# Two heads' small products alternate between the halves of TensorE's array, and a low part is laid out on all rows

## The chip, the cores and the metric

The kernel runs on one core of one Trainium2 chip. The metric is device time in microseconds of one launch, weights read from HBM included. Everything is float32 at the interface. TensorE's array has 128 rows (the contraction) and 128 columns (the outputs' partitions); an instruction whose operands need only 64 rows or 64 columns is placed on one half of the array. A stationary operand is loaded by a weight load (PEld in the profile), and a matmul then streams the moving operand past it.

## The reference

Three transformer blocks for 512 tokens of width 1024. The first two mix three branches, and the third has attention, a delta rule and an expert layer:

```python
def first_block(x, p, ...):
    for i in range(2):
        h = rms_norm(x, norm_g[i]); z = h @ w_in[i]
        y_a = rwkv7_branch(z_a, ...)      # 6 heads of 64
        y_b = dsa_branch(z_b, ...)        # 4 heads, top 128 keys by an index score
        y_c = dilated_branch(z_c, ...)    # 3 groups of 2 heads, banded windows
        x = x + concat(y_a, y_b, y_c) @ w_out[i]
        x = x + sigmoid(rms_norm(x, ple_norm_g[i]) @ ple_w_gate[i]) * (p[i] @ ple_w_proj[i])
    return rms_norm(x, final_norm_g)

def second_block(x, c, ...):
    h = rmsnorm(x, n1) * (1 + sc1) + sh1
    # block_attention: softmax(q k^T / 8) v, 8 query heads on 2 key heads of 64
    # gated_delta_chunked: 8 heads of 64, forward and backward; per chunk (k b)(k^T) and q k^T
    x = x + gt1 * ((gate_a * (attn @ w_attn_up) + gate_d * (dn @ w_dn_up)) @ w_o)
    return x + gt2 * expert_choice_ffn(...)   # 16 experts, 64 tokens each
```

Every head has 64 features, so a score product contracts over 64 rows, and P V makes 64 output rows.

## The kernel before

Two heads share one tile of 128 partitions: head e = 0 lies on partitions 0 to 63 and head e = 1 on 64 to 127. Scores of a head therefore use 64 rows of the array (the half that belongs to the head), and P V, which contracts over 128 keys, writes 64 partitions and uses 64 columns (again the head's half).

The places that the change touches:

- `emit_rwkv` (L493), first branch, six times (two layers, three head pairs): Gram products of keys, 64 rows, 256 moving columns, four matmuls for each of two sources and two chunk pairs.
- `emit_dil` (L655, L656), three groups, four blocks, two heads: scores, then a mask added through an identity in bfloat16. `dil_out` (L706) makes the P V of the same.
- `emit_dsa` (L622, L623, L630): the same with 128 to 512 keys.
- `emit_delta` (L1075): Gram products of the delta rule, four times (p = 0 to 3, a pair of heads each).
- `emit_gqa` (L1208, L1209, L1216): grouped attention, one chunk of two query heads for each p; for each of four blocks of 128 tokens and each head, the scores in two passes (the keys' high part on all rows against the query's high and low part, then the keys' low part on the head's own 64 rows), softmax, four transposes (`attend`, L607) and four P V products.

A float32 matmul is two passes in the trace, each with a weight load of its own; a float32r one (scores of the grouped attention, `K.mm` at L199) is one, and so is a transpose. The order of instructions on each engine is made by a scheduler from the order of the code, the dependencies and the pools' buffers: `emit_delta` calls `between(p)` after the solver's code, and the scheduler merges the grouped attention and the gates' projections (L199) with the solver (`K.solve`, L323, L362), whose float16 products come four at a time, and with the delta rule's state chain behind it (L1109 to L1149). Score tiles `bs`, outputs `bo`, Gram tiles `bg` and transposes `bt` have two PSUM buffers each.

The expert weights' loads wait for marks that stand behind the attention and the delta rule:

```python
d = self.nc.sync.dma_start(t, src)
if first:
    self.after(d, self.mark if self.wmn < NE + NW + NM1 else self.mark2)
```

Of the kernel before, what the change touches and what calls it, by code (L numbers as in the profile page):

```python
# [8 lines left out]
F32 = mybir.dt.float32  # L9
F32R = mybir.dt.float32r  # L10
BF16 = mybir.dt.bfloat16
# [3 lines left out]
ALU = mybir.AluOpType  # L15
# [20 lines left out]
# first-block feature-major chunk order  # L36
C_IQ, C_IK, C_WD, C_RK, C_DQ, C_DG, C_DIL = 0, 2, 3, 4, 16, 18, 20
# column offsets in the constants
# [12 lines left out]
# per-partition vectors of a layer  # L51
# [15 lines left out]
class Block:  # L67
# [33 lines left out]
    def small(self, tag, n, bufs=1):  # L101
        """a [128, n] piece of one tile that holds the short vectors, round robin per tag"""
# [8 lines left out]
    def load_x(self, src, mark=None):  # L111
        """the residual stream, token-major: from DRAM"""
# [12 lines left out]
    def load_c(self, g, t):  # L125
        """constants of one phase; the other phase's take the same place"""
        self.cst[g] = t[:, 0:_CSTS[g]]
        self.nc.scalar.dma_start(self.cst[g], self.a[g])
# [4 lines left out]
    def dense(self, lhs, src, out, bytok=False):  # L133
        """token-major products of a feature-major lhs [k][128, 512] with src [1024, 1024], by halves of its columns;
        out(t, hf, psum); the second half, and with bytok the first, goes token tile by token tile"""
# [31 lines left out]
    # ---- weights: one ring of [128, 1024] tiles  # L167
# [10 lines left out]
    def w(self, src, k=1, name="w", bufs=NS, mark=None):  # L178
        """a [128, 1024] tile of weights (seen as k blocks of columns) in two parts"""
# [4 lines left out]
    def split(self, pool, t, name, shape=(128, 512), eng=None, bufs=None, mark=None):  # L184
        """t = hi + lo exactly, both of the tensor engine's single-pass float32 width"""
# [10 lines left out]
    def mm(self, out, a, b, start, stop):  # L196
        """out += a^T b for operands in two parts"""
# [3 lines left out]
    def wm(self, src, pool):  # L201
        """expert weights: the ring and what the earlier phases have left"""
# [20 lines left out]
    def sumsq(self, sp, t, hf):  # L223
        """sum of squares of half a row tile of the residual stream"""
# [8 lines left out]
    def rstd(self, t):  # L233
        """1 / sqrt(mean of squares + 1e-6) of the rows of tile t"""
# [7 lines left out]
    def row(self, lp, src, name, mark=None):  # L242
        """a row of 1024 on all partitions"""
# [6 lines left out]
    def norm_T(self, sp, hp, scale, bias=None, rs=None):  # L250
        """the rows x * rstd * scale + bias transposed, in two parts: [k][128, 512]"""
# [16 lines left out]
    def tpose(self, src):  # L268
        """four [128, 128] blocks transposed"""
# [5 lines left out]
    def fm(self, hT, wt, pool=None):  # L275
        """a feature-major chunk of a projection: [128 features, 512 tokens] in PSUM"""
# [5 lines left out]
    def rope_fm(self, sp, b, cos, sin, mask, out, perm=None, half=None, scale=1.0):  # L282
        """out = (b * cos + shuffled(b) * sin) * scale; half: one half of b's rows for both halves of out"""
# [16 lines left out]
    def rsqrt(self, out, src, scale, bias):  # L300
        """1 / sqrt(src * scale + bias)"""
# [3 lines left out]
    def silu2(self, out, src, sp, tag, n=512):  # L305
        """out = 2 * silu(src)"""
# [4 lines left out]
    # ---- (I + A)^-1 R for strictly triangular A, four units at a time  # L311
# [1316 lines left out]
```

## Time and profile before

| | |
|---|---|
| runs | median 2271.3 us of 3 (2269.49 to 2281.24) |
| profiled execution, span | 2273.9 us |
| TensorE busy | 2128.9 us, 94% of the span |
| VectorE, ScalarE, GpSimd busy | 1258.6, 980.0, 429.6 us |
| granted TensorE clock, mean | 0.973 of full speed |

The profiled execution is known by its span alone, and that lies 2.6 us above the median of the runs and inside their range. Busy shares are of the whole span; the stages differ, so a change is weighed with the rows of the stage in which it lies. A matmul's duration in the trace includes the time in which its results drain, so the cost of one in a stream is the distance from its start to the next one's start. Where several of one kind follow each other, the timeline gives one row for them, with the first start and the number.

### The profile page before, as it was taken

How to read it: one execution, taken by the hardware profiler on the slowest of the kernel's cores; microseconds unless marked ns; L12 is line 12 of the kernel's file. 1: busy time of each engine (PE TensorE's matmuls, PEld its weight loads, DVE VectorE, ACT ScalarE, POOL GpSimd, SP SyncE). 2: the span in 40 equal slices, each digit the busy share in tenths (PEclk: the TensorE clock that was granted, in tenths of full speed). 3: DMA queues.
4: the chain of work that ended last, by engine and by line, in shares of the span. 5: the costliest groups of instructions: out<-in, count | busy, mean ns of one | idle time of the engine just before them, and what ended most of it. 6: DMA issues, size and time to landing. Idle time of an engine off the chain costs nothing. (4 is left out here: it accounts for less than half of the span.)

```text
span 2273.9 us, 31807 instructions
## 1 busy us (share of the span) xinstructions
PE 2128.9 (94%) x12273; PEld 1439.3 (63%) x12273; DVE 1258.6 (55%) x2406; ACT 980.0 (43%) x1849; POOL 429.6 (19%) x344
## 2 busy tenths in 40 slices
PE   6998999999999899999899999999999799999999
PEld 6754667668886676668767777676677444444443
DVE  5688855655569877645867474757464322222221
ACT  4454545444544464444577584857532011101110
POOL 2132233112222323202141140323110000000000
PEclk9999999899999999999999999999999799999999
DMA  6254251043321111034210202011146699999996
GB/s 203 84 171 146 77 168 57 18 158 107 94 87 38 38 38 47 22 124 153 73 51 31 73 20 75 24 61 43 52 157 257 263 401 409 409 409 409 409 409 267
DMA packets 114335, 348.48 MB, mean 153 GB/s; under 512 B 19820, under 2 KB 20604, under 8 KB 114184
## 3 DMA queue, kind: packets, MB, share of 16 engines
q1 hardware_dynamic: 110152, 340.51, 40.7%
q10 hardware_dynamic: 4032, 5.95, 0.8%
q8 instruction: 97, 1.59, 0.3%
q14 instruction: 54, 0.44, 0.1%
HBM read 332.70 MB, written 10.56 MB: 151 GB/s over the span
## 5 line engine op out<-in xcount | busy, mean ns | idle before, releaser
L193 POOL TENSOR_TENSOR wL<-wring,wH 128x1024 fp32r<-128x1024 f32 x68 | 167.2, 2459 | 702.0 <-ACT wH L190 498.8
L190 ACT ACTIVATE wH<-wring 128x1024 fp32r<-128x1024 f32 x137 | 144.1, 1059 | 133.5 <-PE bm L199 96.5
L1387 PE MATMUL bm<-wm,xe 128*64 128x512 f32 x848 | 185.4, 593 | 0.0
L199 PE MATMUL bm<-hT0H,wH 128*128 128x512 f32 x380 | 158.7, 418 | 2.9 <-ACT wH L190 2.9
L199 PE MATMUL bm<-hT1L,wH 128*128 128x512 f32 x380 | 159.8, 421 | 0.0
L199 PE MATMUL bm<-hT0L,wH 128*128 128x512 f32 x380 | 159.6, 420 | 0.0
L199 PE MATMUL bm<-hT0H,wL 128*128 128x512 f32 x380 | 158.6, 417 | 0.0
L199 PE MATMUL bm<-hT1H,wL 128*128 128x512 f32 x380 | 156.5, 412 | 0.0
L199 PE MATMUL bm<-hT1H,wH 128*128 128x512 f32 x380 | 156.0, 411 | 0.0
L1387 PEld LDWEIGHTS bm<-wm,xe 128*64 128x64 f32 x848 | 75.2, 136 | 106.4 <-issue 99.6
L193 DVE TENSOR_TENSOR wL<-wring,wH 128x1024 fp32r<-128x1024 f32 x69 | 92.2, 1337 | 74.4 <-ACT wH L190 66.4
L344 DVE TENSOR_TENSOR Z<-bz,perm 128x512 f16<-128x512 f32 x168 | 108.6, 684 | 36.7 <-PE bz L323 35.6
L1364 DVE TENSOR_SCALAR OH<-phA,perm 128x64 f32<-128x64 f32 x128 | 30.2, 309 | 136.4 <-PE bz L1375 105.7
L1387 PE MATMUL bm<-wm,aT 128*64 128x512 f32 x432 | 102.3, 602 | 0.7
L354 ACT ACTIVATE XX<-bz 128x512 f16<-128x512 f32 x168 | 101.3, 610 | 3.6 <-PE bz L323 3.6
L323 PEld LDWEIGHTS <-XX 128*128 128x128 f16 x1008 | 63.6, 99 | 59.5 <-issue 27.9
L351 ACT ACTIVATE XX<-bz 128x512 f16<-128x512 f32 x140 | 85.2, 608 | 16.7 <-PE bz L323 14.9
L199 PEld LDWEIGHTS bm<-hT0H,wH 128*128 128x128 f32 x380 | 72.8, 192 | 19.4 <-issue 4.2
L199 PEld LDWEIGHTS bm<-hT0L,wH 128*128 128x128 f32 x380 | 72.6, 191 | 17.5 <-issue 5.7
L199 PEld LDWEIGHTS bm<-hT1L,wH 128*128 128x128 f32 x380 | 71.9, 189 | 18.2 <-issue 5.9
L199 PEld LDWEIGHTS bm<-hT1H,wL 128*128 128x128 f32 x380 | 71.9, 189 | 18.1 <-issue 5.3
L199 PEld LDWEIGHTS bm<-hT0H,wL 128*128 128x128 f32 x380 | 72.6, 191 | 15.5 <-issue 3.3
(815 smaller groups left out, 4922.6 us busy)
## 6 DMA issues: line engine op xcount, KB each, us to landing
wm<-in_w_up SPq DMA_DIRECT2D x112, 512.0 KB
wm<-in_w_down SPq DMA_DIRECT2D x108, 512.0 KB
wm<-in_w_gate SPq DMA_DIRECT2D x100, 512.0 KB
wring<-in_win SPq DMA_DIRECT2D x95, 512.0 KB
wring<-in_w_ada SPq DMA_DIRECT2D x48, 512.0 KB
wring<-in_w_gate SPq DMA_DIRECT2D x20, 512.0 KB
wring<-in_w_down SPq DMA_DIRECT2D x20, 512.0 KB
wring<-in_w_out SPq DMA_DIRECT2D x16, 512.0 KB
```

The costliest lines, as they stand in the source:

```text
L190: d = self.A.activation(out=hi, in_=t, func=AF.Copy)
L193: (eng or self.V).tensor_tensor(out=lo, in0=t, in1=hi.bitcast(F32), op=ALU.subtract)
L199: self.T.matmul(out, a[i], b[j], start=(start and n == 0), stop=(stop and n == 2))
L323: T.matmul(b[:, u], lhs[:, u], rhs if len(rhs.shape) == 2 else rhs[:, u], start=True, stop=True)
L344: V.tensor_tensor(out=z, in0=mm(HL[j][0], X[j]), in1=lv(systems[j], l, 0), op=ALU.mult)
L351: A.activation(out=X[j], in_=mm(XT[j], Z[j]), func=AF.Copy)
L354: A.activation(out=XT[j], in_=b, func=AF.Copy)
L1364: V.tensor_scalar(out=y[:, t, 64 * e:64 * e + 64], in0=K.c("iota")[:, 1:65], scalar1=slot[:, t, x:x + 1], scalar2=scale(t, x), op0=ALU.is_ ...
L1387: T.matmul(bb[hf][s], lhs[:, k, s], w[:, hf * 512:(hf + 1) * 512], start=(k == 0), stop=(k == 7))
```

## The change

In all six places the products of the two heads are written alternately (head 0, head 1, head 0, head 1), each on its half of the array; where a score tile was taken for one head at a time, two are taken at once, and P V of both heads stands behind both heads' transposes. In the grouped attention the keys' low part is copied to all 128 rows, one tile per head, and the second pass multiplies it with the query's high and low part on 128 rows, where it used the head's own 64. Comments and doc strings are gone as well, which shifts line numbers.

```diff
@@ emit_rwkv
-                for h in range(2):
-                    b = K.pg.tile([128, 2, 256], F32, name="bg", bufs=2)
-                    for j in range(2):
-                        T.matmul(b[:, j], src[64 * h:64 * h + 64, c0 + j], AR[64 * h:64 * h + 64, c0 + j], start=True, stop=True)
+                bb = [K.pg.tile([128, 2, 256], F32, name="bg", bufs=2) for h in range(2)]
+                for j in range(2):
+                    for b, s in zip(bb, HS):
+                        T.matmul(b[:, j], src[s, c0 + j], AR[s, c0 + j], start=True, stop=True)
+                for h, b in enumerate(bb):
...
+HS = [slice(64 * e, 64 * e + 64) for e in range(2)]
...
@@ emit_dsa
+            ps = [K.ps.tile([128, 512], F32, name="bs", bufs=2)[:, :w] for e in range(2)]
+            for e, s in enumerate(HS):
+                T.matmul(ps[e], q[hp][s, b * 128:(b + 1) * 128], k[s, 0:w], start=True, stop=False)
+            for e in range(2):
+                T.matmul(ps[e], K.identb, am[b][:, :w] if b else K.msk["caus"], start=False, stop=True)
+            PT = []
             for e in range(2):
-                s = slice(64 * e, 64 * e + 64)
-                p = K.ps.tile([128, 512], F32, name="bs", bufs=2)
-                T.matmul(p[:, :w], q[hp][s, b * 128:(b + 1) * 128], k[s, 0:w], start=True, stop=False)
-                T.matmul(p[:, :w], K.identb, am[b][:, :w] if b else K.msk["caus"], start=False, stop=True)
...
-                softmax_parts(K, sp, p[:, :w], w, P, l)
+                softmax_parts(K, sp, ps[e], w, P, l)
...
-                PT = attend(K, sp, P, w, l)
-                for j in range(b + 1):
-                    T.matmul(o[s, b], v[:, j, 0:64], PT[:, j], start=(j == 0), stop=(j == b), skip_group_check=True)
+                PT.append(attend(K, sp, P, w, l))
+            for j in range(b + 1):
+                for e, s in enumerate(HS):
+                    T.matmul(o[s, b], v[:, j, 0:64], PT[e][:, j], start=(j == 0), stop=(j == b), skip_group_check=True)
@@ emit_dil: its scores as in emit_dsa; dil_out
-            for e in range(2):
-                s = slice(64 * e, 64 * e + 64)
-                n = 256 if g == 0 and w else 128
-                PT = attend(K, sp, P[g, w, e], n, mx[:, g, 2 * w + e:2 * w + e + 1])
-                for j in range(n // 128):
-                    T.matmul(o[s, w], v[g][:, w - n // 128 + 1 + j, s], PT[:, j], start=(j == 0), stop=(j == n // 128 - 1),
+            n = 256 if g == 0 and w else 128
+            PT = [attend(K, sp, P[g, w, e], n, mx[:, g, 2 * w + e:2 * w + e + 1]) for e in range(2)]
+            for j in range(n // 128):
+                for e, s in enumerate(HS):
+                    T.matmul(o[s, w], v[g][:, w - n // 128 + 1 + j, s], PT[e][:, j], start=(j == 0), stop=(j == n // 128 - 1),
@@ emit_delta
-        for e in range(2):
-            s = slice(64 * e, 64 * e + 64)
-            for c0 in (0, 2):
-                b = K.pg.tile([128, 2, 2, 128], F32, name="bg", bufs=2)
-                for j in range(2):
+        for c0 in (0, 2):
+            bb = [K.pg.tile([128, 2, 2, 128], F32, name="bg", bufs=2) for e in range(2)]
+            for j in range(2):
+                for b, s in zip(bb, HS):
                     T.matmul(b[:, j].rearrange("p a b -> p (a b)"), KQ[s, c0 + j, 0:128], KQ[s, c0 + j], start=True, stop=True)
+            for e, b in enumerate(bb):
@@ emit_gqa
-    kl = lp.tile([128, 512], F32R, name="akl")
+    kl = [lp.tile([128, 512], F32R, name="akl%d" % e) for e in range(2)]
...
-        V.tensor_tensor(out=kl[s], in0=k[s], in1=kh[e][s].bitcast(F32), op=ALU.subtract)
+        for x in hs:
+            V.tensor_tensor(out=kl[e][x], in0=k[s], in1=kh[e][s].bitcast(F32), op=ALU.subtract)
...
-                T.matmul(b, q[e][s, ts], kl[s], start=False, stop=True)
+                T.matmul(b, q[e][:, ts], kl[e], start=False, stop=True)
...
-                PT = attend(K, sp, P, 512, l)
-                for j in range(4):
-                    T.matmul(o[s, ts], tmv[:, j, s], PT[:, j], start=(j == 0), stop=(j == 3), skip_group_check=True)
+                PT.append(attend(K, sp, P, 512, l))
+            for j in range(4):
+                for e, s in enumerate(hs):
+                    T.matmul(o[s, ts], tmv[:, j, s], PT[e][:, j], start=(j == 0), stop=(j == 3), skip_group_check=True)
```

The scheduler makes a new order of the whole program from this, on every engine. What stands on TensorE in the grouped attention of the first pair, behind the solver, before (PT is a head's transposed probabilities, one number per head and block; L199 is a projection, L607 a transpose):

```order
L607 MATMUL bt_11242<-perm_82,P_11237 128x128
L1216 MATMUL bo_11138<-PT_11228,tmv_9871 64x128 x4
L607 MATMUL bt_11242<-perm_82,P_11237 128x128 x3
L199 MATMUL bm_11396<-hT0H_9774,wH_11392 128x512
L199 MATMUL bm_11396<-hT0L_9775,wH_11392 128x512
L607 MATMUL bt_11261<-perm_82,P_11256 128x128 x4
L199 MATMUL bm_11396<-hT0H_9774,wL_11393 128x512
L199 MATMUL bm_11396<-hT0H_9774,wH_11392 128x512
L1216 MATMUL bo_11138<-PT_11247,tmv_9871 64x128 x4
```

At the same stage of the changed program (L1225 is P V, L611 a transpose, L1216 and L1217 the two score passes, L1115 and L1124 the delta rule's state chain, L1139 its product with GDb):

```order
L1115 MATMUL bg_11463<-dkd_10403,dW_10401 128x128 x2
L1225 MATMUL bo_11141<-PT_11208,tmv_9871 64x128
L1225 MATMUL bo_11141<-PT_11193,tmv_9871 64x128
L1225 MATMUL bo_11141<-PT_11208,tmv_9871 64x128
L1225 MATMUL bo_11141<-PT_11193,tmv_9871 64x128
L1225 MATMUL bo_11141<-PT_11208,tmv_9871 64x128
L1225 MATMUL bo_11141<-PT_11193,tmv_9871 64x128
L1225 MATMUL bo_11141<-PT_11208,tmv_9871 64x128
L1216 MATMUL bs_11256<-akh0_10041,aq0_11135 128x512
L1217 MATMUL bs_11256<-akl0_10043,aq0_11135 128x512
L1124 MATMUL bg_11470<-dU_10402,dkd_10403 128x128
L611 MATMUL bt_11226<-perm_82,P_11221 128x128 x4
```

Before, the four P V products of one head stood together, with other work on the whole array between the heads. Now seven of the eight of a block stand together and change heads at each one (the eighth, of head 0, was placed ahead), and they stand in the midst of the delta rule's state chain.

The first scores of the dilated attention on TensorE, before (L655 scores, L656 the mask and its weight load):

```order
L655 MATMUL bs_3102<-lk0_2803,lq0_2765 128x128
L656 LDWEIGHTS perm_82
L656 MATMUL bs_3102<-perm_82 128x128
L655 MATMUL bs_3107<-lk0_2803,lq0_2765 128x128
L656 LDWEIGHTS perm_82
L656 MATMUL bs_3107<-perm_82 128x128
```

The same place of the changed program:

```order
L661 MATMUL bs_3102<-lk0_2803,lq0_2765 128x128
L661 MATMUL bs_3103<-lk0_2803,lq0_2765 128x128
L663 LDWEIGHTS perm_82
L663 MATMUL bs_3102<-perm_82 128x128
L663 LDWEIGHTS perm_82
L663 MATMUL bs_3103<-perm_82 128x128
```

The two score products, each on its half of the rows, now follow each other, and the two masks come behind.

## Rows read from the trace of the kernel before

**Rows 1.** The page: busy time of the engines

```profile
PE 2128.9 (94%) x12273; PEld 1439.3 (63%) x12273; DVE 1258.6 (55%) x2406; ACT 980.0 (43%) x1849; POOL 429.6 (19%) x344
```

**Rows 2.** Stretches: us, busy us (instructions) of PE, PEld, DVE, ACT, POOL, clock, DMA

```profile
360.00:420.00 60.00, 60.00 (x404) 43.49 (x403) 41.08 (x99) 35.42 (x86) 13.51 (x11) 1.00 0.14 37
1205.00:1260.00 55.00, 53.34 (x495) 40.30 (x495) 35.42 (x67) 39.46 (x79) 12.10 (x12) 1.00 0.12 39
1455.00:1515.00 60.00, 59.71 (x543) 45.84 (x541) 37.11 (x73) 40.73 (x82) 10.50 (x11) 1.00 0.14 47
```

**Rows 3.** Who TensorE waited for in 1180 to 1640 us, longest in total

```profile
PE bz L323 <- DVE XX L338: 8.7, 7, 3.5
```

**Rows 4.** Groups of instructions, shapes kept apart: busy us, mean ns

```profile
L1216 PE MATMUL bo<-PT,tmv 128*64 128x128 f32 x256 | 38.2, 282 | 0.2
```

**Rows 5.** Timeline of TensorE: start us, us, line, tiles, stationary rows*columns

```profile
1257.06 0.39 PE L199 MATMUL bm<-hT0H,wL 128*128 128x512 f32 x1
1257.38 1.09 PE L1216 MATMUL bo<-PT,tmv 128*64 128x128 f32 x8
1258.39 0.50 PE L199 MATMUL bm<-hT1H,wH 128*128 128x512 f32 x1
1258.74 0.40 PE L199 MATMUL bm<-hT1L,wH 128*128 128x512 f32 x1
```

**Rows 6.** Timeline of TensorE, where the outputs of a delta pair are made

```profile
1271.56 0.66 PE L1149 MATMUL bg<-GDb,dU 128*64 128x128 f32 x8
1272.15 0.49 PE L1144 MATMUL bg<-dQT,dNN 128*128 128x128 f32 x2
```

**Rows 7.** Timeline of TensorE, Gram products of the first branch

```profile
125.28 1.14 PE L493 MATMUL bg<-AR,bh 64*128 64x256 f32 x8
126.35 1.02 PE L918 MATMUL bm<-wring,perm 128*1 128x512 f32 x2
```

**Rows 8.** Timeline of TensorE, Gram products of the delta rule

```profile
1181.42 0.39 PE L199 MATMUL bm<-hT0H,wH 128*128 128x512 f32 x1
1181.65 0.40 PE L199 MATMUL bm<-hT0L,wH 128*128 128x512 f32 x1
1181.97 1.13 PE L1075 MATMUL bg<-KQ 64*128 64x256 f32 x4
1183.03 0.50 PE L199 MATMUL bm<-hT0H,wL 128*128 128x512 f32 x1
1183.37 0.40 PE L199 MATMUL bm<-hT0H,wH 128*128 128x512 f32 x1
```

**Rows 9.** Timeline of TensorE, grouped scores inside the solver

```profile
1210.36 0.38 PE L323 MATMUL bz<-Z,XX 128*128 128x128 f16 x4
1210.67 0.49 PE L1209 MATMUL bs<-akl,aq 64*128 64x512 f32 x1
1211.09 0.40 PE L323 MATMUL bz<-XX,Z 128*128 128x128 f16 x4
1211.30 0.48 PE L1208 MATMUL bs<-akh,aq 128*128 128x512 f32 x1
1211.62 0.40 PE L323 MATMUL bz<-XX,HL 128*128 128x128 f16 x4
```

**Rows 10.** Timeline of TensorE, P V inside the solver

```profile
1219.35 0.40 PE L323 MATMUL bz<-Z,XX 128*128 128x128 f16 x4
1219.68 0.43 PE L1216 MATMUL bo<-PT,tmv 128*64 128x128 f32 x2
1220.05 0.40 PE L323 MATMUL bz<-XX,Z 128*128 128x128 f16 x4
1220.28 0.39 PE L323 MATMUL bz<-Z,XX 128*128 128x128 f16 x4
```

**Rows 11.** The lower copy of the grouped keys: one tile's instructions (ns min/median/max)

```profile
L1193 DVE TENSOR_TENSOR akl<-araw,akh x2: 684/688/691, 1148.5 to 1150.4; 64x512 fp32r<-64x512 f32 x2
```

**Rows 12.** One stretch: us, busy us of the engines, clock, DMA

```profile
426.80:443.90 17.10, 17.10 (x47) 7.64 (x46) 5.21 (x15) 5.07 (x16) 0.00 (x0) 0.50 0.00 0
```

More of the change, by code (lines that the diff above doesn't have):

```diff
@@ L649, in emit_dil @@
         for w in range(4):
-            for e in range(2):
-                s = slice(64 * e, 64 * e + 64)
-                p = K.ps.tile([128, 512], F32, name="bs", bufs=2)
-                j0 = (w - 1) * 128 if g == 0 and w else w * 128
-                n = (w + 1) * 128 - j0
-                T.matmul(p[:, :n], q[g][s, w * 128:(w + 1) * 128], k[g][s, j0:j0 + n], start=True, stop=False)
-                T.matmul(p[:, :n], K.identb, K.msk["band" if n == 256 else "blkcaus" if g == 2 else "caus"], start=False, stop=True)
-                sm = p[:, :n]
+            j0 = (w - 1) * 128 if g == 0 and w else w * 128
+            n = (w + 1) * 128 - j0
+            ps = [K.ps.tile([128, 512], F32, name="bs", bufs=2)[:, :n] for e in range(2)]
+            for e, s in enumerate(HS):
+                T.matmul(ps[e], q[g][s, w * 128:(w + 1) * 128], k[g][s, j0:j0 + n], start=True, stop=False)
+            for e in range(2):
+                T.matmul(ps[e], K.identb, K.msk["band" if n == 256 else "blkcaus" if g == 2 else "caus"], start=False, stop=True)
+            for e, sm in enumerate(ps):
                 x = g * 8 + w * 2 + e
@@ L700, in dil_out @@
         for w in range(4):
-            for e in range(2):
-                s = slice(64 * e, 64 * e + 64)
-                n = 256 if g == 0 and w else 128
-                PT = attend(K, sp, P[g, w, e], n, mx[:, g, 2 * w + e:2 * w + e + 1])
-                for j in range(n // 128):
-                    T.matmul(o[s, w], v[g][:, w - n // 128 + 1 + j, s], PT[:, j], start=(j == 0), stop=(j == n // 128 - 1),
+            n = 256 if g == 0 and w else 128
+            PT = [attend(K, sp, P[g, w, e], n, mx[:, g, 2 * w + e:2 * w + e + 1]) for e in range(2)]
+            for j in range(n // 128):
+                for e, s in enumerate(HS):
+                    T.matmul(o[s, w], v[g][:, w - n // 128 + 1 + j, s], PT[e][:, j], start=(j == 0), stop=(j == n // 128 - 1),
                              skip_group_check=True)
@@ L1204, in chunk @@
         for t in range(4):
-            for e, s in enumerate(hs):
+            ts = slice(t * 128, (t + 1) * 128)
+            PT = []
+            for e in range(2):
                 b = K.ps.tile([128, 512], F32, name="bs", bufs=2)
-                ts = slice(t * 128, (t + 1) * 128)
                 T.matmul(b, q[e][:, ts], kh[e], start=True, stop=False)
-                T.matmul(b, q[e][s, ts], kl[s], start=False, stop=True)
+                T.matmul(b, q[e][:, ts], kl[e], start=False, stop=True)
                 P = sp.tile([128, 512], F32, name="P")
```

1 line of the change is left out of this document (removed).

## Prediction

> **What bounds the kernel now.** I read the page first: TensorE is busy for 94% of the span, VectorE for 55% [rows 1]. Then the stretches in which the change lies: the dilated scores (360 to 420 us), and the grouped attention inside and behind the solver (1205 to 1260 and 1455 to 1515 us). There TensorE is busy for 97 to 100% of the time at full clock, while VectorE and ScalarE have a quarter or more of it free [rows 2]. Third, the waits of TensorE over all four pairs of the delta rule: the longest of 460 us adds up to 8.7 us, and it is the solver's own [rows 3]. So in these stages time on TensorE is time of the kernel, and what the change takes off its queue moves all that follows. The tail moves along: the expert weights' loads wait for marks that stand behind the attention.
>
> **What two halves cost alone and together.** Timelines show it, by the distance between starts. Eight passes of P V of one head (four products of two passes) take 1.02 us [rows 5]. The delta rule already makes its outputs alternately on the two column halves: there eight passes of the same shape take 0.59 us [rows 6]. So a pair of products, one on each half, saves (1.02 - 0.59) / 2 = 0.215 us; that is two passes of some 0.11 us. For the row halves: four passes of 256 columns of one head take 1.06 us [rows 8], and eight passes of the first branch's Gram products 1.07 us [rows 7]. So a pair of 256 columns saves two passes of 0.215 us, 0.43 us, and of 128 columns half of it, 0.215 us.
>
> Rows 7 say something else as well. They are of the program before, where the order has two products of head 0 and then two of head 1. That they take the time of four passes means that the queue already puts them side by side without alternation. So alternating the products in emit_rwkv is worth nothing: 22 of its 26 stretches have this form.
>
> **What a change of half costs.** Going from whole to half and back costs as well. Between L199 products, which follow each other at 0.23 us [rows 8], the one ahead of P V takes 0.32 and the one behind it 0.35, and the eight passes 1.02 where 8 x 0.11 is 0.88: 0.09 + 0.12 + 0.14 = 0.35 us for a stretch on column halves [rows 5]. Between solver products it is (0.33 + 0.37) - (0.23 + 2 x 0.11) = 0.25 us [rows 10]. I take 0.3. On row halves: 0.32 ahead, 0.34 behind, 1.06 for 4 x 0.215 = 0.86: 0.09 + 0.11 + 0.20 = 0.40 us [rows 8]; between solver products some 0.30, so 0.35.
>
> **The change, part by part.** The numbers of products and of stretches (runs of instructions on half the array) are counted over the whole order of both programs; what stands next to each other there is not always what the code writes next to each other.
>
> 1. Grouped P V: 128 products, 256 passes [rows 4]. Before, none has the other head beside it. After, 43 pairs have (of 64: the scheduler puts some products of head 0 ahead alone). 43 x 0.215 = 9.2 us.
> 2. P V of the sparse and the dilated attention: 24 pairs before, 48 after: 24 x 0.215 = 5.2 us.
> 3. Dilated scores: no pair before, 10 after, 6 of them with 256 columns: 6 x 0.43 + 4 x 0.215 = 3.4 us. Sparse scores: 2 pairs of 128 columns, 0.4 us. The other 28 and 28 stay alone, since a score buffer frees at a time and the scheduler fills the time between.
> 4. Gram products of the delta rule: 2 pairs before, none after, since the second Gram buffer comes free later and other work is put between: a loss of 0.9 us.
> 5. The grouped scores' second pass. On 64 rows between two solver groups it stretches their distance to 0.73 us (1210.36 to 1211.09); the first pass, on all rows, to 0.53 us (1211.09 to 1211.62) [rows 9]. The second pass now has the first one's form: 0.20 us each, 32 of them, 6.4 us.
> 6. Stretches, without those 32: on column halves 7 fewer, on row halves 4 fewer (dilated scores -10, sparse -2, Gram +6, the delta rule's gates +2): 7 x 0.3 + 4 x 0.35 = 3.5 us.
> 7. Added: two more subtractions of 64 x 512 for the low part, 0.69 us each on VectorE, once, at 1148 to 1150 us [rows 11]. The first second pass starts at 1210.67 us [rows 9], so 60 us of other work hide them; uncovered they would cost 1.4 us. The softmax work of VectorE and ScalarE and all DMAs keep their number and size.
>
> Sum: 9.2 + 5.2 + 3.4 + 0.4 - 0.9 + 6.4 + 3.5 = 27.2 us less on TensorE. P V of head 0 now waits behind the softmax of head 1; where 460 us of the fullest stage show 8.7 us for the longest wait [rows 3], I allow 2 us for new ones. So 25 us: a span of 2273.9 - 25 = 2249 us, and 2271.3 - 25 = 2246 us against the median of the runs, which lies 2.6 us lower than this execution.
>
> **A rule that speaks against it.** P V pairs share all 128 rows and differ in columns alone, and eight alternating passes take 0.59 us against 1.02 [rows 5, 6]. The Trainium skill ("TensorE: Matmul & The Clock Gate", Part 3, "The mechanism") says that a weight load overlaps running matmuls only when its row group differs. By that rule two column halves would hinder each other, points 1 and 2 would give nothing, and the sum would be 27.2 - 14.4 = 12.8 us. The trace does not agree with it, and the measurement decides; as a rival it stands below.
>
> **The rivals.**
>
> - *The gain goes into waits in a strict queue.* A block's P V now needs both heads' softmax, scaling, transposes and copy. There are 16 such groups in the grouped, 16 in the sparse and 24 in the dilated attention, 56. If TensorE stands for 0.27 to 0.68 us at each, 15 to 38 us come back, and the time is within 0.5%: some 2260 to 2282, say 2267 us. For it: ScalarE is busy for 39.5 of 55 us there, and its copy is the last step ahead of P V [rows 2]. Against it: the order keeps other work between a head's transposes and its P V nearly everywhere. 0.17.
> - *Slower.* The order moves the grouped attention's later blocks from the solver into the delta rule's state chain: P V, transposes and scores stand between the links of that chain. A P V product whose transposed probabilities are late then holds the chain as well. It decides from 0.7 us at each of the 56 groups (39 us in all, 27 that are gained and 11 more); at 0.9 us it is 50 us, and the time 2271 - 27 + 50 = 2294 us. Against it: before, the chain is covered by projections, which remain as cover. 0.08.
> - *Column halves do not run together for P V*: points 1 and 2 fall away, with the 2 us for waits kept 2271 - 11 = 2260 us, right on the bound between faster and the same. The delta rule's rows speak against it, with the same shape and type [rows 6]. 0.04.
> - *More comes off than counted.* From 426.8 to 443.9 us, in the sparse attention of the first layer, the granted clock is 0.50 (1.2 of 2.4 GHz) for 17.1 us with TensorE always occupied [rows 12]. At full clock the same work takes half, 8.5 us less. What went before is the start of this attention, where half-array products alternate with little else; the new order has more whole-array products between. With that the gain is 34 us, 2237 us; the order may add some 10 us of luck, 2227. The same effect can go the other way by as much elsewhere. 0.10.
>
> **How the numbers follow.** The likeliest, with 0.61, is 25 us less: 2246 us; by itself it has a range of 2236 to 2258 (pairs and stretches at their lower and upper prices, 3 us each way, waits of 0 to 12 us, and the new order of everything else, whose effect no row prices). 0.5%, some 11 us, is about what a measurement of this kernel can tell from no change; the three runs lie 12 us apart. Below 2260: the likeliest's 0.61 with the larger gain's 0.10 and half of the column rival's 0.04, 0.73. Within 0.5%: 0.17 and the other half, 0.19. Slower: 0.08. The range must leave out no more than 0.2: from 2220 (the larger gain almost whole) to 2274 (most of the waits rival), which leaves 0.03 below and some 0.13 above.
>
> **What would show it right or wrong.** In the profile after: TensorE's busy time lower by some 25 us and its share still 93 to 94%. The P V group of the grouped attention (256 passes) falls from 38.2 us [rows 4] to about 29, with starts a few ns apart for the two heads. The second pass has 128 rows, and a solver group around it a distance of 0.53 us. The four delta pairs follow each other some 4 us sooner. The Gram products of emit_rwkv keep 1.07 us for eight passes. If the waits on ACT PT ahead of P V sum to over 15 us, the first rival holds; if the state chain's links are further apart, the second. The prediction is wrong in its base if TensorE's busy time falls by 25 us and the span does not.

## The result, and the profile after

The changed kernel runs in 2299.7 us (median of 4, 2298.8 to 2300.8), beside the kernel before in 2276.3 us on the same chip: a ratio of 1.0096, 95% interval 1.0066 to 1.0125. It is slower by 1%, where 25 us less were forecast.

The page of the changed kernel, its span and the engines' busy time, answers [rows 1]:

```profile
span 2297.0 us, 31862 instructions
PE 2126.7 (93%) x12269; PEld 1428.0 (62%) x12273; DVE 1265.5 (55%) x2408; ACT 977.3 (43%) x1849; POOL 427.2 (19%) x344
```

TensorE is busy for as long as before, to 2 us. Three numbers take this apart, and they are used for every run below. Idle time is the span less the busy time: 2297.0 - 2126.7 = 170.3 us, before 2273.9 - 2128.9 = 145.0. Time at half clock (0.50, 1.2 of 2.4 GHz) follows from the mean granted clock, 0.965 now and 0.973 before: 2 x (1 - 0.965) x 2297.0 = 161 us against 123. Half of that is time lost, so TensorE's work at full clock is 2126.7 - 80 = 2046 us now, and 2128.9 - 62 = 2067 before (an estimate: it takes TensorE as busy in all of the half-clock time, and the clock has three decimals, worth 1 us of work). The work did fall, by 21 us. Idle time took 25 us back, and the clock 19.

The products themselves cost about what was counted. The grouped P V by its group (busy us, mean ns) answers [rows 4]:

```profile
L1225 PE MATMUL bo<-PT,tmv 128*64 128x128 f32 x256 | 25.7, 284 | 0.9 <-ACT PT L613 0.9
```

The second pass and a P V stretch in the timeline of TensorE (start us, us) answer [rows 5, 9]:

```profile
1257.69 0.39 PE L323 MATMUL bz<-XX,Z 128*128 128x128 f16 x4
1257.89 0.48 PE L1217 MATMUL bs<-akl,aq 128*128 128x512 f32 x1
1258.21 0.40 PE L323 MATMUL bz<-Z,XX 128*128 128x128 f16 x4
...
1282.96 1.09 PE L1225 MATMUL bo<-PT,tmv 128*64 128x128 f32 x14
1283.98 0.50 PE L1216 MATMUL bs<-akh,aq 128*128 128x512 f32 x1
```

Fourteen passes of P V now take 1.02 us from start to start (1282.96 to 1283.98), where eight did [rows 5]; the group falls from 38.2 to 25.7 us. The second pass has 128 rows, and the solver groups around it start 0.52 us apart (1257.69 to 1258.21), where it was 0.73 [rows 9].

So where did it go? Rows of stretches show it, first of the kernel before, then of the changed one (columns as in [rows 2]): the program up to the first dilated score, the attention over selected keys of the second layer (from its first score to the last dilated P V behind it), the stretch from there to the delta rule, and the four pairs of the delta rule.

```profile
0.00:365.80 365.80, 322.80 (x1906) 228.74 (x1906) 248.89 (x473) 165.29 (x288) 99.08 (x83) 0.96 0.42 139
948.00:1015.80 67.80, 65.48 (x337) 39.35 (x337) 29.39 (x65) 31.38 (x86) 8.92 (x5) 0.97 0.21 77
1015.80:1180.00 164.20, 153.41 (x728) 121.17 (x725) 107.37 (x175) 93.93 (x166) 37.55 (x18) 0.97 0.32 107
1180.00:1726.00 546.00, 520.90 (x3638) 385.38 (x3638) 341.10 (x603) 335.90 (x608) 140.34 (x134) 0.99 0.20 68
```

```profile
0.00:378.00 378.00, 328.57 (x1880) 229.85 (x1881) 251.12 (x471) 164.30 (x283) 98.77 (x83) 0.94 0.41 135
956.70:1036.90 80.20, 73.70 (x333) 41.20 (x335) 29.01 (x65) 30.12 (x85) 5.00 (x4) 0.83 0.15 58
1036.90:1211.80 174.90, 162.46 (x749) 126.19 (x747) 111.25 (x176) 100.42 (x171) 41.81 (x19) 0.96 0.32 107
1211.80:1747.70 535.90, 504.06 (x3621) 373.13 (x3620) 342.91 (x604) 333.05 (x607) 134.91 (x134) 0.98 0.20 67
```

The attention over selected keys has as many instructions as before, within 1%, and takes 12 us more, at a mean clock of 0.83: (1 - 0.83) x 80.2 = 13.6 us of it are the clock's, where 2.0 were. The four pairs of the delta rule take 535.9 us where the kernel before takes 546.0: there the change pays, 10 us, though idle time rises from 25.1 to 31.8 us. The first dilated score starts at 378 us and not at 366: 12 us are lost where, of all edits, only the first block's Gram loop lies. The stretch ahead of the delta rule holds no edit on TensorE and takes 11 us more, in part since 21 more of TensorE's instructions stand in it.

### The profile page after: what moved, and what is told of

Its sections match the earlier page's. It is cut to its first block, busy times and chain, and to the rows that moved or that the text cites. A ratio compares the mean times of both kernels' runs of the same rounds, so it can differ in the third digit from the quotient of the medians.

```text
span 2297.0 us, 31862 instructions
## 1 busy us (share of the span) xinstructions
PE 2126.7 (93%) x12269; PEld 1428.0 (62%) x12273; DVE 1265.5 (55%) x2408; ACT 977.3 (43%) x1849; POOL 427.2 (19%) x344
## 5 line engine op out<-in xcount | busy, mean ns | idle before, releaser
L199 PE MATMUL bm<-hT0H,wH 128*128 128x512 f32 x380 | 158.0, 416 | 3.6 <-ACT wH L190 3.3
L199 PE MATMUL bm<-hT1L,wH 128*128 128x512 f32 x380 | 160.0, 421 | 0.0
L199 PE MATMUL bm<-hT0H,wL 128*128 128x512 f32 x380 | 159.3, 419 | 0.6 <-DVE wL L193 0.5
L199 PE MATMUL bm<-hT0L,wH 128*128 128x512 f32 x380 | 158.8, 418 | 0.0
L199 PE MATMUL bm<-hT1H,wH 128*128 128x512 f32 x380 | 156.7, 412 | 0.0
L199 PE MATMUL bm<-hT1H,wL 128*128 128x512 f32 x380 | 156.4, 411 | 0.0
L613 ACT ACTIVATE PT<-bt 128x128 f32<-128x128 f32 (+3 forms) x112 | 46.4, 429 | 124.6 <-PE bt L611 117.9
L199 PEld LDWEIGHTS bm<-hT0H,wH 128*128 128x128 f32 x380 | 72.6, 191 | 19.9 <-ACT wH L190 4.3
L199 PEld LDWEIGHTS bm<-hT0L,wH 128*128 128x128 f32 x380 | 72.8, 192 | 17.3 <-issue 5.4
L199 PEld LDWEIGHTS bm<-hT0H,wL 128*128 128x128 f32 x380 | 72.7, 191 | 17.3 <-issue 4.4
L199 PEld LDWEIGHTS bm<-hT1L,wH 128*128 128x128 f32 x380 | 72.0, 190 | 16.9 <-issue 4.8
```

Source lines behind the costliest of these rows:

```text
L199: self.T.matmul(out, a[i], b[j], start=(start and n == 0), stop=(stop and n == 2))
L613: K.A.activation(out=PT[:, :n], in_=b[:, :n], func=AF.Copy)
```

## The experiments

The theories, as the expectations name them. A: the prices of the prediction hold; the loss comes from the order that the scheduler gives to everything else, since it sets the order of the whole program anew after any edit. B: P V that waits for both heads' softmax holds TensorE's queue. C: the alternating Gram products cost in themselves (two PSUM buffers taken at once, products torn apart). D: alternation costs in any order, by its waits. E: what is taken off in the attention stages was cover for the softmax chains, that is, work which TensorE did while VectorE and ScalarE made the probabilities. Times are medians, with the ratio to the kernel before in the same session and its interval. Idle, half-clock time and work are of the profiled execution, worked out as above; it lies up to 8 us from the median (e2, e3, e4, e8). The expectations price a stretch on half the array at some 0.22 us, where the prediction had 0.3 to 0.35.

| run | us | ratio | idle | half clock | work |
|---|---|---|---|---|---|
| before | 2273 | | 145 | 123 | 2067 |
| changed | 2300 | 1.0096 [1.0066, 1.0125] | 170 | 161 | 2046 |
| e1 first block's Gram alone | 2282 | 1.0031 [1.0012, 1.0050] | 149 | 123 | 2072 |
| e2 delta Gram alone | 2279 | 1.0020 [0.9997, 1.0043] | 142 | 132 | 2063 |
| e3 low parts alone | 2252 | 0.9900 [0.9855, 0.9944] | 137 | 131 | 2055 |
| e4 grouped P V alone | 2281 | 1.0024 [1.0007, 1.0042] | 158 | 114 | 2071 |
| e12 first block's scores, P V alone | 2253 | 0.9900 [0.9866, 0.9934] | 134 | 122 | 2057 |
| e10 all but Gram | 2236 | 0.9835 [0.9802, 0.9867] | 139 | 112 | 2042 |
| e15 all but first block's Gram | 2290 | 1.0048 [1.0020, 1.0076] | 160 | 165 | 2046 |
| e16 all but delta Gram | 2307 | 1.0140 [1.0095, 1.0185] | 173 | 185 | 2045 |
| e5 all, order of before | 2271 | 0.9987 [0.9970, 1.0004] | 188 | 164 | 2002 |
| e7 all, order of e3 | 2247 | 0.9884 [0.9851, 0.9918] | 173 | 130 | 2004 |
| e11 as e7, no selected keys | 2250 | 0.9895 [0.9866, 0.9923] | 157 | 148 | 2016 |
| e13 all, order of e10 | 2251 | 0.9898 [0.9862, 0.9934] | 158 | 130 | 2025 |
| e6 undone, order of changed | 2332 | 1.0269 [1.0229, 1.0309] | 181 | 159 | 2070 |
| e14 as e10, order of changed | 2314 | 1.0181 [1.0121, 1.0241] | 181 | 190 | 2039 |
| e8 changed, neutral move | 2300 | 1.0108 [1.0072, 1.0145] | 171 | 184 | 2043 |
| e9 before, neutral move | 2276 | 1.0007 [0.9988, 1.0025] | 145 | 132 | 2066 |
| e17 order of changed, then good | 2333 | 1.0226 [1.0168, 1.0283] | 198 | 214 | 2026 |
| e18 good, then order of changed | 2296 | 1.0084 [1.0055, 1.0114] | 172 | 156 | 2043 |

### Parts alone (e1 to e4, e12)

Each is the kernel before with one part of the diff: the Gram loop of emit_rwkv (e1), of emit_delta (e2), the low parts on all rows (e3), the grouped P V (e4), emit_dsa with emit_dil and dil_out (e12).

> The kernel before with one part of the change alone: the Gram products of the first branch alternate. In the order of this kernel, counted on TensorE as in the prediction, the part is worth about -4 us (a loss: two pairs fewer, six row stretches more), and the first 470 instructions of TensorE are those of the kernel before. Theory A (the prices of the prediction hold, and the loss of the full change comes from the scheduler's new order in stages that no edit touches): the first 85 us as before to 0.5 us, the stages behind differ by several us either way, the whole within 1% of before, no better than the count. Theory B (the loss comes from coupling two heads' softmax ahead of P V): within 0.3% of before. Theory C (the loss comes from the Gram products): slower by 10 us or more, all of it in the first 366 us and in 690 to 880 us.

> The kernel before with the Gram products of the delta rule alternating, and nothing else. Counted: about -0.4 us (a small loss). Its edit lies behind 1180 us, yet its order on TensorE departs from that of the kernel before at instruction 329, in the first branch. Theory A: the first 1000 us, which hold no edit, change by 3 us or more somewhere, and the whole by up to 1% either way. Theories B and C: the first 1000 us as before to 1 us, the whole within 0.3% (B) or slower by up to 5 us in the four delta stages (C).

> The kernel before with the keys' low part on all rows and the second pass of the grouped scores on 128 rows, and nothing else. Counted: 6.4 us less for the pass, some 2 us lost on stretches and pairs elsewhere, 4.6 us in all. Theory A: the pass between two solver groups takes 0.53 us instead of 0.73, the four delta stages win, but the whole lies anywhere from 20 us faster to 15 us slower, since the order departs at instruction 329. Theories B and C: 2 to 8 us faster, all of it behind 1180 us.

> The kernel before with the grouped P V of both heads alternating behind both heads' transposes, and nothing else. Counted: about 7.6 us less on TensorE. Theory A: the grouped stages (behind 1180 us) win, the first 1000 us, without an edit, change by several us, the whole within 1% of before. Theory B: the delta stages get longer by 5 us or more in all, with waits of P V on the copy of the transposed probabilities, and the whole is slower. Theory C: 5 to 8 us faster.

> The edits of the two attentions of the first block alone (scores and P V of selected keys and of the dilated groups), in the order that the scheduler gives. Counted against before: 10 us of half-array products and 19 stretches fewer, 14 us. Theory A: 2259 us plus or minus 15 by the order's idle and half-clock time. Theory E: idle time in the two stages of the selected keys rises from 4 us to 10 or more, and the total stays within 5 us of 2273.

e3 and e12 are 21 and 20 us faster, more than the 5 and 14 us counted for them; e1, e2 and e4 are 6 to 9 us slower. Added up the five give -19 us, and the whole change +23. The three of the attentions (e3, e4, e12) add up to -34 us and run together as e10 below in -37: it is with the Gram loops that the sum breaks. So no part holds the loss by itself: not B (in e4 the delta rule with the grouped attention, to its last product, gets shorter, 458.0 us for 465.9, and grouped P V waits 0.6 us in all), not E alone (idle time falls in e12), and not C as stated. Stages that an edit does not touch moved too, which spoke for A. The edit of e2 lies behind 1180 us, yet the first layer's attention over selected keys takes 60.8 us for 68.9. In e4 the selected keys are as before, by heads, and their P V waits 5.3 us for the copy of its transposes, where none waits in the kernel before and 5.6 us in the changed one (us, times, longest; first e4, then the changed kernel):

```profile
PE bo L631 <- ACT PT L610: 5.3, 10, 0.7
```

```profile
PE bo L637 <- ACT PT L613: 5.6, 11, 0.7
```

So these waits come with an order, without alternation there.

### One order forced on other products (e5 to e7), and neutral moves (e8, e9)

To part order from products, a table of one program's order (`o`) is laid over another program's instructions (`by[e]`) on TensorE and on VectorE, with edges that need no semaphore; ScalarE, GpSimd and the DMAs stay with the scheduler. Products that the change pairs are laid together.

```python
    info = mybir.DependencyInfo(mybir.DependencyClass.NoSync, mybir.DependencyReason.DATA)
...
        for a, b in zip(o, o[1:]):
            tc.add_manual_dep(by[e][b], by[e][a].name, info, reason="order")
```

> The whole change, but TensorE's and VectorE's instructions stand in the order of the kernel before, apart from the alternating products themselves, which stand together in pairs where the first (scores, Gram) or the second head's (P V) stood. Edges without a semaphore between neighbours on the engine hold that order. Counted against the kernel before: about 46 us of half-array products fewer and 131 half-array stretches fewer (at the prediction's price of some 0.22 us a stretch, 29 us), so 75 us less TensorE work, against 33 counted for the changed kernel as scheduled. Theory A (the loss lies in the new order of everything that is not edited): under 2235 us, near 2200 if no new wait takes the gain. Theory D (the alternation itself costs: a pair waits for the later of two softmax chains, and the queue waits with it): over 2265 us in this order too, with idle time of TensorE some 20 us or more over the 145 of before.

> The kernel before, nothing alternated and the second pass on half the rows, but TensorE's and VectorE's instructions stand in the order that they have in the changed kernel, apart from the products that the change pairs, whose heads stand one after the other. Counted against the changed kernel: 18 us of half-array products and 24 stretches more, 24 us. The tile of transposed probabilities has two buffers. Theory A: 2300 + 24, so 2310 to 2335 us: slower than before by 2 per cent though no product is other than before. Theory D: the pairs' waits are gone, so it is near before, 2265 to 2285 us.

> As the whole change in the order of before, but in the order that the scheduler gave the kernel with the low-part edit alone, which ran in 2252 us, 16 us better than its counted work explains. Theory A: an order keeps its worth, so this is some 15 us under the whole change in the order of before, and under 2215 us. Theory D: over 2240 us. If orders have no worth of their own, it is within 5 us of the whole change in the order of before.

e6 is the clearest: products as before, in the changed kernel's order, 2332 us, 60 us over the kernel before, by idle time (+36) and clock (+18), with the same work to 3 us. In one and the same order, undoing the alternation costs 32 us: 24 of work, as counted, and 11 of idle time. So alternation pays what was counted, and the order loses more. e5 shows another side, where A missed: with every pair together in the old order, TensorE's work falls by 65 us (75 were counted) and the time by nothing. The page of e5, and who TensorE waited for there in the second layer's attention over selected keys (us, times, longest):

```profile
PE 2083.6 (92%) x12273; PEld 1416.8 (62%) x12273; DVE 1250.2 (55%) x2408; ACT 977.8 (43%) x1849; POOL 430.9 (19%) x344
```

```profile
PE bt L611 <- ACT PT L613: 7.3, 3, 6.3
PE bt L611 <- DVE P L608: 3.4, 4, 1.5
```

The queue waits for the softmax chain and its copy, as D says, where an order made for other products leaves nothing between them. Of the 43 us of new idle time 21 lie in the two attentions over selected keys and 15.5 in the delta rule, up to its last product. e7 has the same products and the same rule of placing in another order, and is 24 us faster. Orders differ in worth with equal work (2002 and 2004 us), but A missed here as well: it had e7 under 2215 us, and D's "over 2240" holds for both.

Then two moves that change no work: the subtractions for the low parts are emitted behind all copies of the high parts, in the changed kernel (e8) and in the kernel before (e9).

```diff
         for x in hs:
             A.activation(out=kh[e][x], in_=k[s], func=AF.Copy)
+    for e, s in enumerate(hs):
         for x in hs:
             V.tensor_tensor(out=kl[e][x], ...)
```

> The changed kernel with one move that changes no work: the four subtractions for the keys' low parts are emitted after the four copies of the high parts and not among them. The scheduler answers with another order of TensorE's instructions (2550 differing rows); the counted work, pairs and stretches are those of the changed kernel to 0.1 us. Theory A: the time moves by 5 us or more to either side of 2300 us, with the difference spread over stages that the move does not touch. Theory D: 2295 to 2305 us.

> The kernel before with a move that changes no work: the two subtractions for the keys' low parts are emitted after the copies of the high parts and not among them. The scheduler gives TensorE another order (2601 differing rows); pairs, stretches and instruction counts stay as they are. Theory A (an order has a worth of its own): 5 us or more away from 2273 us on either side, by idle time and half-clock time of TensorE. If orders are worth nothing unless a product changes: 2268 to 2278 us.

Here A as I had put it is wrong: some 2,600 rows of TensorE's order change, and the time stays at 2300 and at 2276 us. So a new order does not have to cost anything: these two did not.

### Without the Gram edits (e10), and which of them (e13 to e16)

> The whole change without the two edits of Gram products, in the order that the scheduler gives it. Counted against the kernel before: some 19 us of half-array products and 54 stretches fewer, 31 us. Theory A: 2242 us if this order's idle and half-clock time are those of before (145 and 123 us), up to 25 us more if they are those of the changed kernel. Theory C (the Gram edits cost 15 us together, as they did alone): under 2250 us. Theory E (what is taken off in the two attention stages was cover for the softmax chains): idle time of TensorE at 155 us or more with the rise in the stages of the scores with selected keys, 2250 to 2275 us.

> As the whole change in the order of the low-part edit (2247 us, TensorE idle 173 us), but the attention over selected keys is as it was before: scores and P V by heads, not alternated. Counted: 8 us of half-array products and 26 stretches more, 14 us. Theory E: the idle time of the two stages of the selected keys falls from 22 us to 5, so 2240 to 2250 us. Theory A: an order is worth what it is worth and the products add up, so 2258 to 2264 us.

e10 leaves out the two Gram loops alone, and is 37 us faster than before: 25 us less work, 6 us less idle time, and 5 us by the clock (11 us less at half). Of work 31 us were counted, so the products gave less than their prices, and idle time and the clock added 11 us. The result also lies under C's 2250. e11 came as E has it: 12 us of work given back and 16 us of idle time gained (157 for 173 us), 9 us lost by the clock, and no change to e7 beyond 3 us. In that order the pairs of the selected keys take cover from their own softmax chain; in e10's they hardly do, with 5.7 us of idle time in the two stages where the kernel before has 3.7. Is it then the Gram products (C), or the order that comes with them (A)?

> The whole change with both Gram edits, but TensorE and VectorE in the order that the change without Gram edits was given (2236 us), the alternating Gram products together where the first head's stood. Counted work is that of the change without Gram edits or a few us less. Theory A (the order of everything else carries the loss): 2225 to 2250 us. Theory C (the alternating Gram products cost in themselves, by two buffers taken at once or by their place in the queue): 2280 us or more.

> The change without its Gram edits, but TensorE in the order of the whole change, each Gram product by heads at the place of its alternating group. Theory A: 2285 to 2310 us, with idle and half-clock time like those of the changed kernel (170 and 161 us). Theory C: 2230 to 2250 us.

> The whole change without the Gram edit of the first block (RWKV), in the scheduler's order. Counted against before: 22 us of half-array products and 42 stretches fewer less 7 us of full rows, 24 us, so 2249 us if the order is as good as without Gram edits. Theory C, by the first block's Gram products: under 2260 us. If the delta rule's Gram edit is what costs: over 2280 us.

> The whole change without the Gram edit of the delta rule, in the scheduler's order. Counted against before as the changed kernel, 27 us less work, so 2246 us if the order is as good as without Gram edits. If the first block's Gram edit is what costs: over 2280 us. If the loss needs both: both this and the run without the first block's stay under 2265 us.

e13 has both Gram edits in e10's order: 2251 us, 49 us less than the changed kernel with the same products. e14 has none in the changed kernel's order: 2314 us, 78 more than e10. Both lie just above A's ranges (by 1 and 4 us) and far from C's. So the loss goes with the order of TensorE and VectorE: it makes 49 us with the Gram edits and 78 without, where the Gram edits make 15 more in the one order and 14 less in the other. Added to the rest, either Gram edit suffices to bring a bad order about (e15, e16).

Two limits. Not all of the 49 us is the order of other things: by the profiles they are 12 of idle time, 15 of the clock and 21 of work, and of the work 9 are the delta rule's Gram products, which the scheduler tore apart in the changed kernel (17.5 us from start to start, in 19 stretches; 15.5 before) and which are laid together in e13 (8.5 us in 8 stretches). As much of C is true. And no run lays a program's own order over itself, so what the laying costs is not measured; e13 and e14 are each 14 to 15 us slower than the run whose order they took.

The same stretch as above, the second layer's attention over selected keys, first in e10, then in e13, then in e14:

```profile
937.20:999.20 62.00, 59.27 (x334) 35.20 (x334) 28.42 (x64) 29.17 (x84) 6.81 (x4) 1.00 0.20 76
```

```profile
935.50:998.00 62.50, 59.59 (x334) 35.29 (x334) 28.41 (x64) 31.09 (x86) 6.81 (x4) 1.00 0.20 76
```

```profile
964.00:1046.60 82.60, 74.28 (x336) 41.23 (x335) 28.99 (x65) 31.45 (x87) 5.07 (x4) 0.83 0.17 64
```

The stage follows its order, not the Gram edits: 62 us at a clock of 1.00 with or without them, 80 to 83 us at 0.83 likewise. With nothing alternated (e6, same order) it is as long, but by other means, 11.7 us of idle time at a clock of 0.95:

```profile
969.30:1049.00 79.70, 67.96 (x336) 39.23 (x335) 31.38 (x65) 33.40 (x88) 9.19 (x5) 0.95 0.18 61
```

What differs inside shows in the timeline where one pair of heads ends and the next begins; first the changed kernel, then e10.

```profile
977.66 0.87 PE L637 MATMUL bo<-PT,v 128*64 128x128 f32 x10
978.46 0.49 PE L625 MATMUL bs<-dk,dq 64*128 64x128 f32 x2
978.87 0.23 PE L627 MATMUL bs<-perm 128*128 128x128 bf16 x1
979.13 0.63 PE L611 MATMUL bt<-perm,P 128*128 128x128 f32 x4
980.51 0.43 PE L637 MATMUL bo<-PT,v 128*64 128x128 f32 x2 [0.75 <-ACT PT L613]
981.18 0.48 PE L625 MATMUL bs<-dk,dq 64*128 64x128 f32 x2 [0.24 <-ACT P L569]
981.60 0.23 PE L627 MATMUL bs<-perm 128*128 128x128 bf16 x1
981.97 1.11 PE L611 MATMUL bt<-perm,P 128*128 128x128 f32 x4
983.77 0.48 PE L637 MATMUL bo<-PT,v 128*64 128x128 f32 x2 [0.69 <-ACT PT L613]
```

```profile
954.09 0.87 PE L634 MATMUL bo<-PT,v 128*64 128x128 f32 x10
954.89 0.39 PE L624 MATMUL bs<-am,perm 128*128 128x512 bf16 x1
955.21 0.49 PE L622 MATMUL bs<-dk,dq 64*128 64x128 f32 x2
...
955.99 0.60 PE L608 MATMUL bt<-perm,P 128*128 128x128 f32 x4
956.34 0.48 PE L199 MATMUL bm<-wH,yS2H 128*128 128x512 f32 x1
956.66 0.39 PE L199 MATMUL bm<-wL,yS2H 128*128 128x512 f32 x1
956.89 0.39 PE L199 MATMUL bm<-wH,yS2L 128*128 128x512 f32 x1
957.12 0.39 PE L199 MATMUL bm<-wH,yS2H 128*128 128x512 f32 x1
957.35 0.40 PE L199 MATMUL bm<-wL,yS2H 128*128 128x512 f32 x1
957.58 0.40 PE L199 MATMUL bm<-wH,yS2L 128*128 128x512 f32 x1
957.91 0.43 PE L634 MATMUL bo<-PT,v 128*64 128x128 f32 x2
```

In e10 six whole-array products of 512 columns stand between the transposes and the P V that needs their copy. In the changed kernel none does, and TensorE waits 0.75, 0.24 and 0.69 us within 4 us (the view ends within the last row). The clock falls right there, at 981.8 us, after the first two of these waits; stretches of the changed kernel:

```profile
977.00:981.80 4.80, 3.65 (x25) 2.12 (x23) 2.17 (x6) 2.42 (x6) 0.00 (x0) 1.00 0.00 0
981.80:1002.20 20.40, 19.35 (x59) 10.05 (x58) 6.35 (x19) 4.60 (x16) 0.00 (x0) 0.50 0.00 0
```

TensorE is busy for 3.65 of 4.80 us, then 20.4 us are granted at 0.50, though it is busy for 19.35 of them. The idle time of both stretches is 2.2 us, the clock's share 10. The half-clock stretch of [rows 12], in the kernel before, looks alike: TensorE is busy for 4.39 of the 5.60 us ahead of it, with one wait of 1.21 us.

```profile
421.20:426.80 5.60, 4.39 (x19) 2.58 (x19) 5.59 (x17) 3.82 (x8) 2.43 (x1) 1.00 0.11 37
```

There six whole-array products stood in the same 5.60 us (422.28 to 423.86), and the clock fell all the same. And e6 has 5 us more of idle time in the stage than the changed kernel, but 8 us at half clock where that has 27. That the waits bring the clock down is thus possible and not shown.

### Half the program in either order (e17, e18)

> The whole change; TensorE is in the changed kernel's order up to the first product of the second RWKV layer's first head pair, and behind it in the order of the whole change in the good order (2251 us). VectorE is left to the scheduler. By the profiles the changed kernel is 23 us behind that run at the cut and loses 25 us after it. If the loss is local: 2270 to 2278 us, with the stages behind the cut as long as in the good order. If it has one origin early in the program: 2290 us or more. If it lies in the second layer and behind alone: under 2258 us.

> The same cut the other way round: the good order in the first layer, the changed kernel's order behind. If the loss is local: 2272 to 2282 us, with the stage of the selected keys in the second layer near 80 us at half clock for 20 us or more, as in the changed kernel. If it has one origin early in the program: under 2260 us.

Both missed: 2333 us is over 2290, as one early origin would have it, but over the changed kernel too, and 2296 us fits neither case; there is no sum of 23 and 25. VectorE's order was left free here. Of some 40 us of idle time that e17 has over e13, 18 stand in the delta rule behind the cut, where TensorE's order is the good one in both; its longest wait there takes 4.4 us in e13, and in e17:

```profile
PE bg L1036 <- ACT lsq L1034: 19.2, 5, 6.3
```

In e18 the first dilated score comes at 385 us, later than in the changed kernel, though TensorE has the good order there, with which e13 reaches it at 368. So the loss isn't an attribute of TensorE's order alone; how the other queues stand to it counts as well. The stage above follows its own side of the cut in part: 63 us in e17, where the good order holds, and 70 in e18, where near 80 were expected.

## Why the prediction was wrong

- The step that failed is the term for "the new order of everything else, whose effect no row prices". The sum puts it at nothing, and the range of the likeliest case holds it, with everything else, inside some 11 us each way; of the rivals one gives it 10 us of luck, and none a loss. I took edits whose products are worth nothing (point 4, and "alternating the products in emit_rwkv is worth nothing") for edits that do nothing. With either of the two added to the rest, the scheduler gives the whole program another order. In the changed kernel this took 25 us of idle time and 19 us by the clock, against 21 us of work gained; between two orders it makes 49 us (e13 against the changed kernel, 9 of them the delta rule's Gram products) to 78 us (e14 against e10). By the runs the term is larger than all others together, so the range was far too narrow and the chance of 0.08 for slower far too small.
- The products were priced right in kind, and some 6 us too high: in the changed kernel work fell by 21 us of 27.2, in e10 by 25 of 31, with a time 37 us under that of before. The sign that I named for it, a busy time 25 us lower, did not come (2126.7 us for 2128.9), since time at half clock is busy time too.
- Points 1 and 2 (P V pairs): right in kind. The group of 128 products fell by 12.5 us where 9.2 were counted. The rival by which column halves do not run together is excluded: fourteen alternating passes take 1.02 us. The rule that it came from (the Trainium skill, "TensorE: Matmul & The Clock Gate", Part 3, "The mechanism") does not agree with this trace either: the third weight load of these fourteen starts at 1283.02 us, while the first two matmuls, on the same 128 rows, run to 1283.29.
- Point 4 (the delta rule's Gram products): a loss of 2.0 us from start to start, 0.9 were counted. The Gram products of emit_rwkv keep 1.07 us for eight passes, as said.
- Point 5 (second pass): the distance is 0.52 us, as forecast with 0.53.
- "I allow 2 us for new ones": idle time rose by 25 us. The allowance was read from the delta rule [rows 3], where idle time rose by 7; the rest came in the attentions over selected keys (8) and ahead of the first dilated score (6), with smaller amounts elsewhere.
- The clock: I gave [rows 12] a gain, as the order would put whole-array products between. In that stage it came: 6.8 us at half clock in the changed kernel and 3.4 in e10, where 17.1 were. What I had said of elsewhere came too, and larger: in the second layer's stage 27 us for 3, and 161 for 123 in all. My ground for it, the half-array products ahead of that stretch, leaves out a wait of 1.21 us that stands there as well.
- The rival that ended slower had the wrong place: the four pairs of the delta rule got 10 us shorter. The strict queue's rival does not hold in the changed kernel, where P V waits for its copy for 6.5 us in all and not for over 15; in e5 and e7 pairs do wait for the softmax, and e11 gets that back as idle time.

Open is why the scheduler's order with a Gram edit leaves the selected keys without whole-array products between the heads. It wasn't tried to move only those products back. By the profiles the changed kernel loses 25 us to e13 in the two attentions over selected keys (70.0 and 80.2 us, in e13 62.6 and 62.5), 11 ahead of the first dilated score and 10 between the selected keys and the delta rule; the causes inside the last two were not looked for.

## What to carry to other kernels

Where a scheduler orders the whole program, an edit has two prices: its products, which rows of the trace give to some 20%, and the order that it triggers, which no row of the trace before gives. So build the change part by part, leave out the parts whose products are worth nothing, and keep the order of a good version: here all but the two Gram loops gives 2236 us, 1.65% under the kernel before, and the whole change 2300. To tell the two prices apart, run the same products in two orders and two sets of products in the same order; and hold VectorE's order along with TensorE's, since TensorE's alone did not carry a time over (e17, e18).

## What the runs showed of the hardware

- Not expected: in the changed kernel waits of 0.75 and 0.24 us among half-array products were followed by 20.4 us at half clock (0.50), which cost 10 us; in e10, with six whole-array products in their place and no such wait, the same stage stayed at 1.00. What brings the clock down is open: the stage has more idle time and less time at half clock in e5 (15.0 and 14 us) and e6 (11.7 and 8 us) than in the changed kernel (6.5 and 27 us).
- Products on the two column halves, each over all 128 rows, run side by side when they alternate: fourteen passes in 1.02 us, where eight of one half take as long [rows 5].
- Taking 65 us of TensorE's work off with the order otherwise unchanged (e5) gave no time at all: 43 us came back as idle time, and 41 us more were spent at half clock, which costs half of that.
